# A hybrid encoder block on one core: edges that fix the written order of three engines, and tiles at multiples of 64 bytes

## The chip, the cores and the metric

The kernel runs on one core of one Trainium2 chip. The core has TensorE (PE in the profile, with its weight loads as PEld), VectorE (DVE), ScalarE (ACT), GpSimd (POOL) and SyncE (SP); each works through a queue of its own, in the order in which the compiled program lists its instructions, and they wait for each other by semaphores. The metric is the time of one execution on the device in microseconds; lower is better.

## The reference

One encoder layer over 256 positions of width 2048: four mixers side by side (a gated linear attention, a Fourier mixer, a Hyena long convolution and a short convolution), cross-attention to 256 memory rows, a SwiGLU of width 5632, with a norm before each and at the end. Nearly all the work is in the products with the weight matrices.

```python
mem_n = rms_norm(mem, mem_norm_g)
h = rms_norm(x, norm_g[l, 0])
q, k, v, g, lr, u_f, u_h, u_s = jnp.split(h @ w_in[l], split_at, axis=-1)
y_a = gla_mixer(q, k, v, g, lr, ...)
y_b = rms_norm(fnet_mixer(u_f), grp_norm_g[l, 0])
y_c = rms_norm(hyena_mixer(u_h, hy_conv_w[l], filt, hy_skip[l]), grp_norm_g[l, 1])
y_d = rms_norm(shortconv_mixer(u_s, sc_conv_w[l]), grp_norm_g[l, 2])
x = x + jnp.concatenate([y_a, y_b, y_c, y_d], axis=-1) @ w_out[l]
x = x + cross_attention(rms_norm(x, norm_g[l, 1]), mem_n, w_xq[l], w_xkv[l], w_xo[l])
x = x + swiglu(rms_norm(x, norm_g[l, 2]), w_gate_up[l], w_down[l])
return rms_norm(x, final_norm_g)

def cross_attention(h, mem_n, w_q, w_kv, w_o):
    ...
    s = jnp.einsum('bshd,bmhd->bhsm', q, k).astype(jnp.float32) * XA_HD ** -0.5
    p = jax.nn.softmax(s, axis=-1).astype(v.dtype)
    o = jnp.einsum('bhsm,bmhd->bshd', p, v).reshape(bsz, seq, D_MODEL)
    return o @ w_o

def swiglu(h, w_gate_up, w_down):
    gate, up = jnp.split(h @ w_gate_up, 2, axis=-1)
    return (jax.nn.silu(gate) * up) @ w_down
```

## The kernel before

**Numbers in two parts.** Every matrix operand is kept as a high part, rounded to a shorter format (fp32r), and a low part, the remainder. An activation slot (act0 to act23, f0 to f35, oex0 to oex3) is a tile of 128x512: the high part of 256 positions and then the low part. A product of one block of 128x128 weights is two matmuls (mm): the high weights wh with all 512 columns of the slot (L269), then the low weights wl with the 256 high ones (L270). With narrow=True the first is split in two of 256 columns (L266, L267). gemm_rows turns the roles round: the slot is the stationary operand and four blocks of wh or wl, 512 columns, stream (L321 to L323).

**The weight stream.** The blocks lie in DRAM in the order in which they are used. Stream._half takes half a slab, eight blocks: SyncE loads a slab into raw (three buffers), ScalarE casts it to wh (L89), VectorE subtracts to get wl (L90). take() calls _half at the start of every eight blocks, so that two halves more than the one in use are written ahead, or three while the pool wx is open (mixers and attention). With three buffers of wh and wl, or four, the half written then needs the buffers that TensorE has just left.

**The gemms and their order.** w_xkv for the memory's keys and values, w_in for the four mixers, w_out, then in attention() w_xq (one head of 64 blocks after the other) and w_xo, then in mlp() w_gate_up and w_down. A gemm runs over columns of 128; for each, all blocks of the inner dimension, accumulated in a bank of PSUM (psG, four banks; psM has four more for small products), and then evac(): merge() copies one half of the bank on ScalarE (L276) and adds the other on VectorE (L178), and what follows depends on the gemm. The groups that begin a gemm (first) run four or eight columns together.

**The background.** The small work between the gemms (the norms, Hyena's filters and convolutions, the gated attention, the attention heads, the loading of keys and values) is written as Python generators. Background holds them with a clock of its own: pe() adds the time of each block, dve() adds what a step gives VectorE to an account, owed, which TensorE's time pays off. After every block mm() calls poll(), and a generator whose due time has come, while owed is below 0.9, runs to its next yield; there it is due again after what is owed plus 1.3 (LAG) or a time that it names. drain() runs a generator to its end at once. So the text of the program has a definite order: the blocks, and steps of the background between them.

**Who decides the order of the queues.** The tile framework records the instructions in that order, and a scheduler then lists them for each engine. It goes by a model of times: where the next instruction of an engine isn't ready in that model, a later one that is ready may go first. Nothing in the kernel before restrains it.

**Places that the prediction speaks of.** rstd_begin multiplies squares with ones (L215), rstd_cols makes a reciprocal root in small operations on VectorE, rstd_bank scales the identity by it (dg, two operations, L244) and multiplies with ones (L246), rstd_end copies the result (rs or krs, L251). Gla.mix does this for four heads, two heads to a step: rstd_end, then a product into go, for each. head() is one attention head: scores (L637, L638), a softmax for each half of the rows, a yield, transposes (L656), a yield, the products with the values (L664, L665). load_kv fetches keys and values (mr) on GpSimd's queue and casts them (L186, L194); it is written in attention(), and so behind the w_out gemm. start_x scales x for one slot, splits it, and after every fourth multiplies the last four with a narrow matrix (L388).

Of the kernel before, what the change touches and what calls it, by code (L numbers as in the profile page):

```python
# [13 lines left out]
F32 = mybir.dt.float32  # L14
# [8 lines left out]
P = 128  # L23
# [24 lines left out]
V_SCW = 133  # L48
V_B1, V_B2, V_FR = 145, 146, 147
V_NT = 148  # L50
NV = 150

TWO_PI_1 = 6.28125
TWO_PI_2 = float(np.float32(2 * math.pi - 6.28125))
# [92 lines left out]
                self.step(e)  # L147


class Block:  # L150
    def __init__(self, ctx, tc, t):
        self.ctx, self.tc, self.nc, self.t = ctx, tc, tc.nc, t
# [66 lines left out]
    def rstd_cols(self, p, n, keep=None):  # L219

        nc = self.nc
        m = p.shape[1]
        self.bg.dve(0, 8)
        c = keep.tile([P, 24], F32, name=f"krc{next(self.kept)}") if keep else self.rp.tile([P, 24], F32, name="rc", tag="rc")
        y, v, a = (c[:, 8 * i:8 * i + m] for i in range(3))
        nc.vector.tensor_scalar(out=v, in0=p, scalar1=1.0 / n, scalar2=EPS, op0=ALU.mult, op1=ALU.add)

        nc.vector.tensor_scalar(out=a.bitcast(U32), in0=v.bitcast(U32), scalar1=1, scalar2=None, op0=ALU.logical_shift_right)
        nc.vector.tensor_scalar(out=y.bitcast(I32), in0=a.bitcast(I32), scalar1=-1.0, scalar2=float(0x5f3759df),
                                op0=ALU.mult, op1=ALU.add)  # L230
        for _ in range(3):
            self.stt(a, y, -0.5, y, ALU.mult, ALU.mult)
            self.tt(a, a, v, ALU.mult)
            self.stt(y, a, 1.5, y, ALU.add, ALU.mult)
        return y
# [95 lines left out]
    def run(self):  # L331
        nc, cp = self.nc, self.cp
        st = self.st
        self.act = [cp.tile([P, 512], F32R, name=f"act{i}") for i in range(24)]
        self.res = [cp.tile([P, 4, R], F32, name=f"res{i}") for i in range(4)]
        self.resk = lambda i: self.res[i // 4][:, i % 4, :]
        self.vec = cp.tile([P, NV], F32, name="vec")
        self.ones = cp.tile([P, P], F32, name="ones")
        self.ident = cp.tile([P, P], F32, name="ident")
        self.acc = cp.tile([P, R], F32, name="acc")  # L340

        self.kd = nc.dram_tensor("keys", (P, 16 * R), F32, kind="Internal").ap()
        self.vd = nc.dram_tensor("values", (P, 8 * 512), F32, kind="Internal").ap()
        nc.scalar.dma_start(self.vec, self.t["vecs"])
        def load(src, k, n):
            nc.sync.dma_start(self.res[k // 4][:, k % 4:k % 4 + n, :].rearrange("p k r -> p (k r)"),
                              self.t[src][:, k * R:(k + n) * R])

        self.load_x = lambda k, n: load("xT", k, n)

        warm = cp.tile([P, 1], F32, name="warm")
        nc.vector.memset(warm, 1.0)
        nc.scalar.copy(warm, warm)
        load("memT", 0, 1)
        st.after = [lambda: None, lambda: None]
        st.after += [lambda a=a: load("memT", *a) for a in ((1, 1), (2, 1), (3, 1), (4, 1), (5, 1), (6, 2), (8, 2), (10, 2), (12, 2), (14, 2))]
        nc.vector.memset(self.ones, 1.0)
        make_identity(nc, self.ident)
        with self.tc.tile_pool(name="wx", bufs=1) as st.extra:
            self.mixers()  # L360
            self.attention()
        self.mlp()
# [5 lines left out]
    def mixers(self):  # L368
        tc, nc, act = self.tc, self.nc, self.act
# [36 lines left out]
            nc.vector.tensor_reduce(out=c[:, 0:2], in_=c[:, 2:10].rearrange("p (r k) -> p r k", k=4), axis=AX.X, op=ALU.add)  # L406

        def prepare(mid):
            c = [mid.tile([P, 10], F32, name=f"sums{i}") for i in range(2)]
            yield 20  # L410
            yield from squares("mem", c[0])
            self.rcm = self.rstd_cols(c[0][:, 0:2], D, self.cp)
            yield
            self.rsm = self.rstd_end(self.rcm, 0, self.cp)
            self.bg.add(hy.filters())
            nc.sync.dma_start(gl.lrw, self.t["lrw"])
            yield from squares("x", c[1])
            col = self.rstd_cols(c[1][:, 0:2], D)
            yield
            self.rsx = self.rstd_end(col, 0, mid)  # L420
# [126 lines left out]
    def attention(self):  # L547
        tc, nc, act, st = self.tc, self.nc, self.act, self.st
        with tc.tile_pool(name="atp", bufs=1) as atp, tc.tile_pool(name="kp", bufs=1) as kp, \
                tc.tile_pool(name="mp", bufs=5) as mp:  # L550
            oex = [atp.tile([P, 512], F32R, name=f"oex{i}") for i in range(4)]
            pt = [atp.tile([P, 512], F32R, name=f"pt{i}") for i in range(2)]
            qs = atp.tile([P, 2], F32, name="qs")
            o = act[0:8] + oex + act[8:12]
            slot = lambda name, n: kp.tile([P, 512], F32R, name=name, tag=name, bufs=n)
            kv = [([], [], []) for _ in range(4)]

            def ev_q(q, p):
                q.append(slot("q", 8))
                self.split(q[-1], self.merge(p))  # L560

            def scales():

                col = self.rstd_begin([[self.acc]], D)
                nc.vector.tensor_scalar(out=qs, in0=col, scalar1=512 ** -0.5, scalar2=None, op0=ALU.mult)
                yield

            heads = []

            def load_kv():  # L570

                todo = [(hd, what, i) for hd in range(4) for what in range(2) for i in range(4)]
                parts = []

                def fetch():
                    if len(parts) < len(todo):
                        hd, what, i = todo[len(parts)]
                        m = mp.tile([P, R], F32, name="mr", tag="mr")
                        o = (4 * hd + i) * R
                        nc.gpsimd.dma_start(m, (self.vd if what else self.kd)[:, o:o + R])  # L580
                        parts.append(m)

                for _ in range(5):
                    fetch()
                yield 4
                for n, (hd, what, i) in enumerate(todo):
                    while hd > len(heads) + 1:
                        yield
                    if what == 0:
                        kv[hd][0].append(slot("kt", 8))  # L590
                        self.split(kv[hd][0][-1], parts[n])
                    else:
                        if i % 2 == 0:
                            kv[hd][1].append(slot("vh", 4))
                            kv[hd][2].append(slot("vl", 4))
                        c = slice(i % 2 * R, i % 2 * R + R)
                        self.split2(kv[hd][1][-1][:, c], kv[hd][2][-1][:, c], parts[n])
                    fetch()
                    yield 1.0

            def scores(hd, q):
                while len(kv[hd][2]) < 2:
                    yield
                yield
                yield from self.head(q, *kv[hd], pt, o[4 * hd:4 * hd + 4], qs)
                heads.append(hd)

            lp = [list(range(8)), list(range(8, 16))]
            self.bg.add(scales())
            self.bg.add(load_kv())  # L610
            gens = []
            for hd in range(4):
                q = []
                if hd > 1:
                    self.bg.drain(gens[hd - 2], True)
                self.gemm("w_xq", [(4 * hd + i) * P for i in range(4)], self.h2, lambda i, p: ev_q(q, p), first=(4, lp),
                          before=lambda n: n and hd == 0 and self.bg.drain(self.late))
                gens.append(self.bg.add(scores(hd, q)))
            h3 = self.h3 = act[12:24] + act[0:4]

            def ev_o(i, p):
                self.residual(i, p, V_NG + 32 + i, h3[i] if i < 12 else None)
                if i == 12:
                    st.extra = None

            self.gemm("w_xo", [i * P for i in range(16)], o,
                      ev_o,
                      first=(4, [list(range(12)), list(range(12, 16))]), before=lambda n: n == 1 and self.bg.drain())
            self.bg.add(self.rest(h3, 12, V_NG + 32))

    def head(self, q, kt, vh, vl, pt, o, qs):
# [10 lines left out]
        for r in range(2):  # L642
            s = self.merge(ps[r])
            self.tt(s, s, self.rsm, ALU.mult)
            c = self.rp.tile([P, 4], F32, name="rc", tag="sm")
            nc.vector.tensor_reduce(out=c[:, 0:1], in_=s, axis=AX.X, op=ALU.max)
            self.stt(c[:, 1:2], c[:, 0:1], -1.0, qs[:, r:r + 1], ALU.mult, ALU.mult)
            nc.scalar.activation(s, s, AF.Exp, scale=qs[:, r:r + 1], bias=c[:, 1:2], accum_out=c[:, 2:3])
# [591 lines left out]
```

## Time and profile before

| | us |
|---|---|
| median of 3 runs | 1525.95 |
| range of the runs | 1525.63 to 1526.79 |
| profiled execution, its own time | 1526.68 |
| span of the profiled execution, first to last instruction | 1524.6 |
| TensorE without work: to the first matmul | 4.55 |
| TensorE without work: 400 to 800 | 3.75 |
| last matmul begins | 1510.76 |

The differences between the profiled execution and its span are launch and end. In the rows in order of time the columns are start and length in us, engine, line, operation, output and inputs, shape, count, and in brackets the idle time before with what ended it. In the groups by line they are engine, operation, count, busy time, mean length in ns, and idle time before. In the list of waits they are who waited for whom, the total, how often, and the longest. A matmul's length in a row contains what overlaps with its neighbours; the pace is read from start to start.

### The profile page before, as it was taken

How to read it: one execution, taken by the hardware profiler on the slowest of the kernel's cores; microseconds unless marked ns; L12 is line 12 of the kernel's file. 1: busy time of each engine (PE TensorE's matmuls, PEld its weight loads, DVE VectorE, ACT ScalarE, POOL GpSimd, SP SyncE). 2: the span in 40 equal slices, each digit the busy share in tenths (PEclk: the TensorE clock that was granted, in tenths of full speed). 3: DMA queues.
4: the chain of work that ended last, by engine and by line, in shares of the span. 5: the costliest groups of instructions: out<-in, count | busy, mean ns of one | idle time of the engine just before them, and what ended most of it. 6: DMA issues, size and time to landing. Idle time of an engine off the chain costs nothing.

```text
span 1524.6 us, 22257 instructions
## 1 busy us (share of the span) xinstructions
PE 1502.2 (99%) x8788; PEld 1311.2 (86%) x8788; DVE 995.5 (65%) x1532; ACT 787.3 (52%) x1238; POOL 40.0 (3%) x76
## 2 busy tenths in 40 slices
PE   8999999999999999999999999999999999999996
PEld 7887788889999788888888888888888888888885
DVE  6676668678667766867766666666666664555454
ACT  6664555557445655656554444444444444444442
POOL 0100100000002000100000000000000000000000
PEclk9999999999999999999999999999999999999998
DMA  9965554354346555544545555555555555555552
GB/s 353 343 239 190 198 193 166 139 195 159 139 167 241 195 190 182 177 149 166 194 166 193 189 185 185 189 192 194 193 193 186 186 186 190 192 192 180 183 191 83
DMA packets 48808, 290.53 MB, mean 191 GB/s; under 512 B 6173, under 2 KB 7486, under 8 KB 17088
## 3 DMA queue, kind: packets, MB, share of 16 engines
q1 hardware_dynamic: 44912, 279.59, 51.5%
q0 software_dynamic: 3072, 8.39, 1.6%
q8 instruction: 69, 1.13, 0.3%
q10 hardware_dynamic: 720, 1.13, 0.2%
q14 instruction: 35, 0.29, 0.0%
HBM read 282.80 MB, written 6.29 MB: 190 GB/s over the span
## 4 chain that ended last, share of the span: by engine, by line
PE 96%; DVE 1%; DMA 1%; issue 1%; ACT 0%; SPq 0%; POOL 0%; DVEq 0%; POOLq 0%; ACTq 0%
PE pg L269 49%; PE pg L270 28%; PE pg L266 3%; PE pg L267 3%; PE pg L321 3%; PE pg L323 2%; PE pg L322 2%; PE pm L269 1%; PE pm L796 1%; DMA mr<-values 1%; PE pm L664 1%; PE pm L270 0%; PE pm L637 0%; DMA raw<-in_W 0%; DVE wl L90 0%
## 5 line engine op out<-in xcount | busy, mean ns | idle before, releaser
L269 PE MATMUL pg<-act,wh 128*128 128x512 f32 x2680 | 939.7, 394 | 8.3 <-DVE act L182 4.5
L90 DVE TENSOR_TENSOR wl<-raw,wh 128x1024 fp32r<-128x1024 f32 (+1 forms) x507 | 617.0, 1218 | 425.9 <-ACT wh L89 423.6
L270 PE MATMUL pg<-act,wl 128*128 128x256 f32 x3008 | 842.5, 281 | 0.0
L89 ACT CAST wh<-raw 128x1024 fp32r<-128x1024 f32 (+1 forms) x507 | 529.5, 1046 | 589.5 <-PE pg L269 333.4
L269 PEld LDWEIGHTS pg<-act,wh 128*128 128x128 f32 x2680 | 504.7, 188 | 120.7 <-ACT wh L89 4.5
L270 PEld LDWEIGHTS pg<-act,wl 128*128 128x128 f32 x3008 | 566.9, 189 | 2.6 <-issue 2.0
L269 PE MATMUL pg<-f,wh 128*128 128x512 f32 x540 | 191.3, 398 | 0.0
L270 PE MATMUL pg<-f,wl 128*128 128x256 f32 x576 | 161.8, 281 | 0.0
L269 PEld LDWEIGHTS pg<-f,wh 128*128 128x128 f32 x540 | 101.5, 188 | 25.2
L270 PEld LDWEIGHTS pg<-f,wl 128*128 128x128 f32 x576 | 108.8, 189 | 0.0
L266 PE MATMUL pg<-act,wh 128*128 128x256 f32 x328 | 94.8, 289 | 0.0
L267 PE MATMUL pg<-act,wh 128*128 128x256 f32 x328 | 92.1, 281 | 0.0
L178 DVE TENSOR_TENSOR tmp<-pg,tmp 128x256 f32<-128x256 f32 x183 | 76.2, 417 | 5.7 <-ACT tmp L276 5.0
L276 ACT COPY tmp<-pg 128x256 f32<-128x256 f32 x179 | 65.0, 364 | 14.6 <-PE pg L270 14.5
L321 PE MATMUL pg<-wh,act 128*128 128x512 f32 x160 | 66.4, 415 | 0.0
L323 PE MATMUL pg<-wh,act 128*128 128x512 f32 x160 | 63.3, 395 | 0.0
L322 PE MATMUL pg<-wl,act 128*128 128x512 f32 x160 | 62.9, 393 | 0.0
L266 PEld LDWEIGHTS pg<-act,wh 128*128 128x128 f32 x328 | 61.9, 189 | 0.7
L267 PEld LDWEIGHTS pg<-act,wh 128*128 128x128 f32 x328 | 61.9, 189 | 0.3
L178 DVE TENSOR_TENSOR tmp<-tmp,rs 128x256 f32<-128x256 f32 x88 | 37.3, 425 | 2.9
L321 PEld LDWEIGHTS pg<-wh,act 128*128 128x128 f32 x160 | 30.0, 188 | 10.4 <-issue 2.9
L322 PEld LDWEIGHTS pg<-wl,act 128*128 128x128 f32 x160 | 30.1, 188 | 7.5 <-issue 1.0
(233 smaller groups left out, 985.1 us busy)
## 6 DMA issues: line engine op xcount, KB each, us to landing
raw<-in_W SPq DMA_DIRECT2D x247, 1024.0 KB, 4.8
raw<-in_W SPq DMA_DIRECT2D x9, 512.0 KB, 7.3
res<-in_xT SPq DMA_DIRECT2D x8, 512.0 KB, 5.6
k<-in_mem SPq DMA_DIRECT2D x8, 256.0 KB, 9.0
k<-in_x SPq DMA_DIRECT2D x8, 256.0 KB, 8.2
keys<-tmp POOLq DMA_DIRECT2D x16, 128.0 KB, 5.7
values<-tmp POOLq DMA_DIRECT2D x16, 128.0 KB, 2.4
mr<-keys POOLq DMA_DIRECT2D x16, 128.0 KB, 3.5
```

The costliest lines, as they stand in the source:

```text
L89: nc.scalar.copy(wh[:, a:b], r[:, a:b])
L90: nc.vector.tensor_tensor(out=wl[:, a:b], in0=r[:, a:b], in1=wh[:, a:b].bitcast(F32), op=ALU.subtract)
L178: self.nc.vector.tensor_tensor(out=out, in0=a, in1=b, op=op)
L266: self.nc.tensor.matmul(p[:, 0:R], wh, slot[:, 0:R], start=start, stop=False)
L267: self.nc.tensor.matmul(p[:, 0:R], wh, slot[:, R:512], start=False, stop=False)
L269: self.nc.tensor.matmul(p[:, :], wh, slot[:, :], start=start, stop=False)
L270: self.nc.tensor.matmul(p[:, 0:R], wl, slot[:, 0:R], start=False, stop=stop)
L276: self.nc.scalar.copy(t, p[:, R:512])
L321: nc.tensor.matmul(ps[r][:, :], hi, wh, start=k == 0, stop=False)
L322: nc.tensor.matmul(ps[r][:, :], hi, wl, start=False, stop=False)
L323: nc.tensor.matmul(ps[r][:, :], lo, wh, start=False, stop=k == nk - 1)
L664: nc.tensor.matmul(p[:, :], vh[m][:, s], pt[m][:, :], start=m == 0, stop=False)
```

## The change

in_order() walks over the recorded instructions once, after the whole program has been written and before the scheduler runs. For TensorE, VectorE and ScalarE it adds an edge from each instruction to the one before it on the same engine, of a class that orders the list at compile time and makes no semaphore. The queues of GpSimd and SyncE get no such edges. DMAs that ScalarE issues count as its instructions.

The sizes of the tiles that were no multiples of 64 bytes for each partition are rounded up: vec from 600 to 640 bytes, the tiles of the reciprocal roots from 96 to 128, warm from 4 to 64, sums from 40 to 64, qs from 8 to 64, the softmax's small tile from 16 to 64. What is computed and the code around are the same.

```diff
-NV = 150
+NV = 160
...
+def in_order(tc):
+
+    last = {}
+    for i in tc.nc.cur_bb.bb.instructions:
+        e = str(i.engine)
+        if any(n in e for n in ("PE", "DVE", "Activation")):
+            if e in last:
+                tc.add_manual_dep(i, last[e].name, mybir.DependencyInfo(mybir.DependencyClass.NoSync, mybir.DependencyReason.DATA),
+                                  reason="order")
+            last[e] = i
...
-        c = keep.tile([P, 24], F32, name=f"krc{next(self.kept)}") if keep else self.rp.tile([P, 24], F32, name="rc", tag="rc")
+        c = keep.tile([P, 32], F32, name=f"krc{next(self.kept)}") if keep else self.rp.tile([P, 32], F32, name="rc", tag="rc")
...
-        warm = cp.tile([P, 1], F32, name="warm")
+        warm = cp.tile([P, 16], F32, name="warm")[:, 0:1]
...
-            c = [mid.tile([P, 10], F32, name=f"sums{i}") for i in range(2)]
+            c = [mid.tile([P, 16], F32, name=f"sums{i}") for i in range(2)]
...
-            qs = atp.tile([P, 2], F32, name="qs")
+            qs = atp.tile([P, 16], F32, name="qs")[:, 0:2]
...
-            c = self.rp.tile([P, 4], F32, name="rc", tag="sm")
+            c = self.rp.tile([P, 16], F32, name="rc", tag="sm")
...
         blk = Block(ctx, tc, t)
+        in_order(tc)
```

## The prediction

> **What bounds the kernel now.** I read the page's busy times first, then TensorE's list of waits, then the rows in order of time around each wait and around each matmul that does not belong to the weight stream.
>
> ```profile
> PE 1502.2 (99%) x8788; PEld 1311.2 (86%) x8788; DVE 995.5 (65%) x1532; ACT 787.3 (52%) x1238; POOL 40.0 (3%) x76
> ```
>
> ```profile
> PE pg L269 <- DVE act L182: 4.5, 1, 4.5
> PE pg L269 <- DVE tmp L178: 3.7, 1, 3.7
> PE pm L711 <- ACT tmp L701: 0.5, 1, 0.5
> PE pm L269 <- ACT wh L89: 0.5, 1, 0.5
> ```
>
> TensorE works for 1502.2 of 1524.6 us. It waits 4.5 us for its first operand, once 3.7 us in the middle, and hardly elsewhere; the other idle time is the tail, from the last matmul (1510.76) to 1524.6. So nothing that makes VectorE or ScalarE faster helps, and every new wait of TensorE lengthens the run by its whole length.
>
> The 3.7 us wait lies in the gemm over w_out. Its rows on ScalarE, then TensorE's:
>
> ```profile
> 495.94 0.40 ACT L194 CAST vh<-mr 128x256 fp32r<-128x256 f32 x1 [3.02 <-DMA mr<-values]
> ...
> 497.81 0.36 ACT L276 COPY tmp<-pg 128x256 f32<-128x256 f32 x1
> ```
>
> ```profile
> 494.69 0.39 PE L269 MATMUL pg<-act,wh 128*128 128x512 f32 x1
> 494.92 0.28 PE L270 MATMUL pg<-act,wl 128*128 128x256 f32 x1
> 498.94 0.79 PE L269 MATMUL pg<-act,wh 128*128 128x512 f32 x1 [3.73 <-DVE tmp L178]
> ...
> 504.67 0.40 PE L269 MATMUL pg<-act,wh 128*128 128x512 f32 x1
> ```
>
> All four banks of psG were full. The copy that begins to empty one (L276) stood in ScalarE's queue behind casts of keys and values (L186, L194), which waited for their DMA. Those casts are written in attention(), after the whole w_out gemm: the scheduler had moved them forward. After the wait TensorE ran at half its pace, a block each 0.64 us instead of 0.347, until 504.22.
>
> The second thing to see is how far VectorE departs from the written order:
>
> ```profile
> 439.07 1.27 DVE L244 TENSOR_SCALAR dg<-ident,rc 128x128 f32<-128x128 f32 x6
> ...
> 445.17 0.88 DVE L182 SCALAR_TENSOR_TENSOR go<-go,vec,rs 128x256 f32<-128x256 f32 x2
> ```
>
> Gla.mix writes, head by head, two dg, the matmul of rstd_bank (L246), the copy to rs, and the product into go. Six dg (three heads) ran 6 us before the first product, so their matmuls found everything ready. The same in Hyena's norm:
>
> ```profile
> 341.18 1.05 ACT L89 CAST wh<-raw 128x1024 fp32r<-128x1024 f32 x1 [1.48 <-PE pg L267]
> 342.16 0.59 PE L246 MATMUL pm<-dg,ones 128*128 128x256 f32 x2
> 342.26 1.22 DVE L90 TENSOR_TENSOR wl<-raw,wh 128x1024 fp32r<-128x1024 f32 x1 [1.57 <-ACT wh L89]
> ```
>
> The dg of this matmul ran at 338.87. By the program's text it comes after the subtraction L90 of 342.26.
>
> **The change, part by part.** The sum is made against the profiled execution, 1526.68 us, of which 1524.6 are the span; the median shown is 1525.95, so differences are added to that.
>
> *The w_out wait goes: -6.5.* In written order the casts for attention come after w_out. From 495.04, where the next block was due, nine blocks at 0.347 would end at 498.17; the trace has 504.67. The 16 casts and subtractions moved into the w_xq gemm (0.33 apart, some 5.3 us of either engine over two heads) are covered there: VectorE is busy 34.28 of 50 us from 550 to 600. Without that cover they would cost those 5.3.
>
> *The starts of tiles: -5.2.* The slots act are the first of their pool and whole multiples of 2048 bytes; f, wh and wl lie behind vec (600 bytes), warm (4) and the tiles of 96 bytes. Matmuls that stream f are slower than those that stream act in the same gemm:
>
> ```profile
> L269 PE MATMUL pg<-f,wh 128*128 128x512 f32 x530 | 187.8, 398 | 0.0
> ...
> L269 PE MATMUL pg<-act,wh 128*128 128x512 f32 x119 | 42.0, 392 | 0.0
> ```
>
> Start to start, a block on f takes 0.3531 us (1292.51 to 1301.69, 26 blocks) and one on act 0.3467 (899.67 to 902.79, nine). If the start is the reason, 576 blocks on f give 576 x 0.0064 = 3.7; the 64 on oex in w_xo 0.4; and the 480 matmuls of gemm_rows, which stream wh and wl at 0.70/3 = 0.2333 against two thirds of 0.3467 = 0.2311, 1.1. Its other bound is 0. I take 5.2, since the tiles that stream slowly are those that lie behind the odd sizes. The Trainium skill (SBUF — State Buffer, Specifications) gives lines of 16 bytes and names no boundary of 64; by it tiles at multiples of 16 would gain nothing and the time be 5.2 later; the rows show a difference of 6 ns, whose reason they do not show.
>
> *L246 waits for its dg: +13.8.* Background takes a step after a block; rstd_bank writes dg and the matmul in the same step. The cast of the next half (L89) and its subtraction (L90) are written at the border of eight blocks, before the step, and the cast waits until TensorE has left the last eight. From the start of that cast it is 1.08 to L90 (341.18 to 342.26), 1.14 to the next operation of VectorE, 0.48 for two dg and 0.37 from VectorE to TensorE (a scaling ended at 606.73, its transposes began at 607.10): 3.1 us. Each matmul now waits 3.1 less its distance from that cast, by the places where TensorE ran it: 63.92 (cast 63.35) 2.5; 97.48 (95.97) 1.6; 342.16 2.1; 443.64 (441.96) 1.4; 449.54 (448.60) 2.2; 464.58 (463.96) 2.5; 783.10 (781.50) 1.5; at 429.31 VectorE is free and nothing is waited for. Behind the waiting matmul stands the whole stream. Bounds: 0, if VectorE comes to dg first as at 429.31, and 9 x 3.1 = 28.
>
> *The second head of a pair: +3.6.* In written order its dg follow the product of the first head, which waits for the copy. From the first matmul 0.63 to its copy (443.64 to 444.27), 0.38, 0.48, 0.48 and 0.37 are 2.3; the first pair of matmuls itself takes 0.5. Two pairs at 1.8.
>
> *Transposes in head(): +7.2.* After its score matmuls the step charges VectorE 2 x (0.42 + 0.42 + 0.16) = 2.0 and is due again 2.0 + 1.3 later, so the transposes are written some 3.4 after the scores' end. Rows 128 to 255 now follow all of rows 0 to 127 on VectorE: twice 0.42 + 0.42 + 0.41 + 0.16 + 0.79 (the exponential on ScalarE with its read) + 0.17 + 0.35 = 2.7 from 601.69, with 0.4 of handovers and the 0.37, is 607.9 against 602.63 + 3.4 = 606.0.
>
> ```profile
> 602.35 0.28 PE L638 MATMUL pm<-kt,q 128*128 128x256 f32 x1
> ...
> 606.52 0.38 PE L656 MATMUL pm<-ident,tmp 128*128 128x128 f32 x2
> 607.10 0.38 PE L656 MATMUL pm<-ident,tmp 128*128 128x128 f32 x2
> ```
>
> Four heads at 1.8; bounds 0 and 4 x 3.
>
> *start_x: +4.4.* The matmuls L388 need the x scaled just before them. VectorE did this early (183.31); as written it follows L90 (183.70, then 1.14), a scaling, cast and subtraction of the slot before: 0.40 + 0.41 + 0.40 more, then 0.48 and 0.37, so 186.9 against 185.63 for the last of them. Four at 1.1; bounds 0 and 8.
>
> *Start and rest: +2.4.* At 7.91 four L269 ran ahead of their L270; now each L270 waits for its wl, 0.4 (0 to 0.7). The other 25 or so places where a background matmul follows VectorE or ScalarE have one or two due times between; I take 2 (0 to 8). The tail has one chain in either order: 0. The edges bring no semaphore: 0.
>
> Sum: -6.5 - 5.2 + 13.8 + 3.6 + 7.2 + 4.4 + 2.4 = +19.7; 1526.68 + 19.7 = 1546.4, or by the median **1546**.
>
> **The rivals.** *VectorE is early enough (faster).* The background's own clock (LAG 1.3, owed below 0.9) spaces dependent steps, and VectorE is idle for 35% of the span. If each first L246 falls late in its eight blocks, at 2.5 of 2.77 us, it waits 0.6: 7 x 0.6 with 3.6 for the pairs is 7.8, against 11.7 gained: 1522; with half of the pairs' wait, 1520. It decides as soon as all waits together stay below 11.7. For it: no bound excludes small waits. Against: of the seven places six lie within 1.7 us of the cast.
>
> *Nothing is reordered.* If the edges do not bind the queues, only the tiles' starts are left: 1521 with their gain, 1526 without. Against it: the six dg above could be nothing but reordered.
>
> *Weights come late (slower still).* In gate_up the evacuation of an odd group now stands before the cast: copy 0.42 after the group's end, three operations of VectorE 0.46 apart to 1.79, a cast, L89 to 3.18, L90 to 4.44; the half is needed 16 x 0.347 = 5.55 after. A chain over 5.55 would cost its excess 44 times; 0.5 of it gives 22 more, 1568. Against: 1.1 us in hand.
>
> *The clock falls at the pairs.* Waits of 1.4 to 2.2 and 1.8 with 0.5 of work between could bring back the half pace, whose eight blocks cost 8 x 0.293 = 2.3 at 499 to 504: 1551 for two. No row has such a pattern, so it stays in the range. The Trainium skill (TensorE: Matmul & The Clock Gate, Why this matters for your kernels) puts the danger at gaps above some 3 us; the row of 3.73 agrees, and by it no single wait here would do it.
>
> **How the numbers follow.** Forecast 0.57, faster rival 0.25, nothing reordered 0.08, late weights 0.10 (the clock within the first). The forecast's own range is 1533 to 1559. For 8 in 10 the whole range goes from 1516, which takes in most of the faster rival, to 1560, leaving late weights and a twentieth at either end out. A measurement tells 0.2%, 3.05 us, from no change: below 1522.9 lie the faster rival and part of the unreordered case, 0.28; within 0.2% 0.07; above 1529.0 0.65.
>
> **What would show it.** Right: TensorE waits at L246 for dg, seven times or more, and at L656 and L388; no wait at w_out's fifth column, and the casts of mr after 573; f and act at the same pace. Wrong: TensorE's waits sum to under 12 us, or its new wait is for wl (L90), or blocks on f still take 0.353.

## The result and the profile after

The changed kernel takes 1595.25 us (median of five runs, 1590.74 to 1598.41) beside 1525.95 us for the kernel before, a ratio of 1.0452 with an interval of 1.0433 to 1.0471. It is 69.3 us slower. The forecast was slower, but 1546 us, and its range ended at 1560.

The profiled execution took 1593.36 us, 1591.5 of them the span. All lines of the changed file behind in_order() are 12 higher than before: L246 is now L258, L244 is L256, L656 is L668, L388 is L400, L269 and L270 are L281 and L282. The busy times of the engines in the kernel after:

```profile
PE 1533.4 (96%) x8788; PEld 1325.8 (83%) x8788; DVE 1012.0 (64%) x1532; ACT 787.8 (49%) x1236; POOL 40.1 (3%) x76
```

TensorE has the same 8788 matmuls, and yet it is busy 31.2 us longer and idle 35.7 us longer (58.1 against 22.4). So there are two losses, not one: it waits more, and it works more slowly while it works. TensorE's list of waits in the kernel after gives the first; its largest lines:

```profile
PE pm L258 <- DVE dg L256: 15.7, 9, 2.1
PE pm L668 <- DVE tmp L662: 9.9, 6, 2.3
PE pm L400 <- DVE tmp L194: 5.9, 7, 1.9
PE pg L281 <- DVE act L194: 5.0, 2, 4.7
PE pg L281 <- ACT wh L89: 3.0, 2, 2.1
PE pg L282 <- DVE wl L90: 1.7, 3, 0.8
...
```

The list has three new lines at the top (dg, transposes, start_x), then the first operand's wait, which was there before, and two lines for weights that come late. What is missing is the wait of 3.7 us for tmp in the w_out gemm. The work of load_kv now stands where it is written. The casts of its tile mr, with shortest, median and longest length in ns and the start of the first and the last, in the kernel before and then in the kernel after:

```profile
L186 ACT CAST kt<-mr x16: 396/407/410, 481.9 to 627.2; 128x256 fp32r<-128x256 f32 x16
L194 ACT CAST vh<-mr x16: 397/405/415, 484.3 to 641.8; 128x256 fp32r<-128x256 f32 x16
```

```profile
L198 ACT CAST kt<-mr x16: 387/400/408, 616.3 to 704.4; 128x256 fp32r<-128x256 f32 x16
L206 ACT CAST vh<-mr x16: 397/401/408, 629.7 to 714.3; 128x256 fp32r<-128x256 f32 x16
```

The second loss has several parts; one of them shows where TensorE waits for nothing. Between 900 and 1000 us both kernels run w_gate_up, only L269 and L270 on act. The windows' rows (length, TensorE's busy time and number of matmuls, granted clock, DMA share, GB/s) are, for the kernel before and then for the kernel after:

```profile
900.00:1000.00 100.00, 100.00 (x579) 1.00 0.53 190
```

```profile
900.00:1000.00 100.00, 100.00 (x572) 1.00 0.53 187
```

At full clock and without a gap, seven matmuls fewer fit into 100 us. Start to start a block (two matmuls) on act takes 0.351 us on the mean where it took 0.347.

### The profile page after: what moved, and what is told of

The parts are those of the page before. It is cut to its first block, busy times and chain, and to the rows that moved or that the text cites. A ratio compares the mean times of both kernels' runs of the same rounds, so it can differ in the third digit from the quotient of the medians.

```text
span 1591.5 us, 22237 instructions
## 1 busy us (share of the span) xinstructions
PE 1533.4 (96%) x8788; PEld 1325.8 (83%) x8788; DVE 1012.0 (64%) x1532; ACT 787.8 (49%) x1236; POOL 40.1 (3%) x76
## 4 chain that ended last, share of the span: by engine, by line
PE 87%; DVE 6%; ACT 4%; issue 2%; DMA 0%; SPq 0%; DVEq 0%; ACTq 0%
PE pg L281 45%; PE pg L282 25%; PE pg L278 3%; PE pg L279 2%; PE pg L333 2%; ACT wh L89 2%; DVE wl L90 2%; PE pg L334 2%; PE pg L335 2%; DVE tmp L190 1%; PE pm L808 1%; PE pm L281 1%; PE pm L258 0%; DMA raw<-in_W 0%; DVE tmp L194 0%
## 5 line engine op out<-in xcount | busy, mean ns | idle before, releaser
L281 PE MATMUL pg<-act,wh 128*128 128x512 f32 x2680 | 953.4, 397 | 5.9 <-DVE act L194 5.0
L282 PE MATMUL pg<-act,wl 128*128 128x256 f32 x3008 | 853.4, 284 | 0.9 <-DVE wl L90 0.9
L90 DVE TENSOR_TENSOR wl<-raw,wh 128x1024 fp32r<-128x1024 f32 (+1 forms) x507 | 606.2, 1217 | 327.4 <-ACT wh L89 326.1
L89 ACT CAST wh<-raw 128x1024 fp32r<-128x1024 f32 (+1 forms) x507 | 519.8, 1040 | 213.8 <-PE pg L281 118.7
L281 PEld LDWEIGHTS pg<-act,wh 128*128 128x128 f32 x2680 | 505.6, 189 | 125.2 <-ACT wh L89 5.9
L282 PEld LDWEIGHTS pg<-act,wl 128*128 128x128 f32 x3008 | 569.2, 189 | 3.4 <-DVE wl L90 2.0
L281 PE MATMUL pg<-f,wh 128*128 128x512 f32 x540 | 193.0, 401 | 2.1 <-ACT wh L89 2.1
L282 PE MATMUL pg<-f,wl 128*128 128x256 f32 x576 | 162.8, 283 | 0.9 <-DVE wl L90 0.8
L281 PEld LDWEIGHTS pg<-f,wh 128*128 128x128 f32 x540 | 102.2, 189 | 27.4 <-ACT wh L89 2.4
L282 PEld LDWEIGHTS pg<-f,wl 128*128 128x128 f32 x576 | 109.7, 190 | 1.6 <-DVE wl L90 1.5
L278 PE MATMUL pg<-act,wh 128*128 128x256 f32 x328 | 96.8, 295 | 0.0
L279 PE MATMUL pg<-act,wh 128*128 128x256 f32 x328 | 93.6, 285 | 0.0
L198 ACT CAST f<-tmp 128x256 fp32r<-128x256 f32 x36 | 14.6, 407 | 50.8 <-DVE tmp L190 50.8
L202 ACT ACTIVATE act<-res,vec 128x256 fp32r<-128x256 f32 x48 | 23.8, 506 | 31.9 <-DVE res L190 31.1
```

The lines of the kernel that those rows point to most:

```text
L89: nc.scalar.copy(wh[:, a:b], r[:, a:b])
L90: nc.vector.tensor_tensor(out=wl[:, a:b], in0=r[:, a:b], in1=wh[:, a:b].bitcast(F32), op=ALU.subtract)
L202: self.nc.scalar.activation(slot[:, 0:R], src, AF.Copy, scale=g)
L278: self.nc.tensor.matmul(p[:, 0:R], wh, slot[:, 0:R], start=start, stop=False)
L279: self.nc.tensor.matmul(p[:, 0:R], wh, slot[:, R:512], start=False, stop=False)
L281: self.nc.tensor.matmul(p[:, :], wh, slot[:, :], start=start, stop=False)
```

## The experiments

Each experiment was timed against runs of the kernel before on the same chip, whose median was between 1526.9 and 1528.0 us.

**The two halves of the change.** edges_only has in_order() and the old sizes; sizes_only has the sizes and not in_order().

```diff
# edges_only
+        in_order(tc)
# sizes_only
-NV = 150
+NV = 160
...
-            qs = atp.tile([P, 2], F32, name="qs")
+            qs = atp.tile([P, 16], F32, name="qs")[:, 0:2]
```

> The edges alone, tiles where they were. Theory A (the edges make TensorE wait, the equal starts of tiles slow its pace): waits at L246, L656 and L388 as after the whole change, some 32 us, and about 10 us of lost clock, less 6.5 for w_out, so 1570 to 1580, with blocks on act still 0.347 apart. Rival B (the starts are a gain, as predicted, and the pace is slow because of the edges): 1597 to 1602, blocks on act at 0.351.

> The tile sizes alone, no edges. Theory A: the weights and the slots now begin at the same place modulo 64 bytes and every block takes 0.351 to 0.353 instead of 0.347: some 3000 blocks x 0.0045 = 13.5 us, 1538 to 1544, the wait in w_out still there. Rival B (the starts as predicted): 1519 to 1523, blocks on f at 0.347. Rival C (no effect): 1526.

Measured: edges_only 1586.96 us (ratio 1.0393, 1.0379 to 1.0407), sizes_only 1536.97 (1.0067, 1.0054 to 1.0079), before 1526.96. The edges cost 60.0 and the sizes 10.0, and their sum of 70.0 is, within the spread of the runs, the whole of the 69.3. Both are losses. The sizes, forecast as a gain, slow the blocks on act from 0.347 to 0.351 us and leave those on f at 0.353.

**The edges engine by engine.** edges_pe orders TensorE alone, edges_dveact VectorE and ScalarE alone.

```diff
# edges_pe
-        if any(n in e for n in ("PE", "DVE", "Activation")):
+        if any(n in e for n in ("PE",)):
# edges_dveact
-        if any(n in e for n in ("PE", "DVE", "Activation")):
+        if any(n in e for n in ("DVE", "Activation")):
```

> Edges on TensorE alone, tiles where they were. If the waits come from VectorE's and ScalarE's order, dg and the like are early again and TensorE waits little at L246 and L656: 1524 to 1534, the wait in w_out still there. If TensorE's own order makes them, about as much as with all edges, 1565 to 1580.

> Edges on VectorE and ScalarE alone, TensorE free to take later blocks first. The casts for attention stay behind w_out, so its wait goes (-6.5). If TensorE's going round is all that keeps it from waiting: 1517 to 1528. If the late dg holds it up in either order: 1535 to 1580.

Measured: edges_pe 1540.18 us (1.0087, 1.0067 to 1.0107), edges_dveact 1562.34 (1.0231, 1.0217 to 1.0245). The largest waits of edges_dveact, and that for dg:

```profile
PE pg L281 <- ACT wh L89: 6.9, 7, 2.1
PE pg L281 <- DVE act L194: 6.0, 3, 4.6
PE pg L282 <- DVE wl L90: 5.1, 8, 0.8
...
PE pm L258 <- DVE dg L256: 0.3, 1, 0.3
```

The wait for dg, 15.8 us with all edges, is 0.3 here and absent in edges_pe: it needs both orders at once. With only VectorE and ScalarE bound, the scheduler let TensorE run weight blocks past the matmul that waits (the second dg of the first pair starts at 68.1, and TensorE runs blocks until its matmul at 68.54). With only TensorE bound, VectorE made dg early, six of them in a row from 439.28 as in the kernel before. The largest waits left with VectorE and ScalarE bound are for weights that come late, 12 us of them. They are not the whole of the 35.4 us: TensorE is idle 15.8 us longer than before and busy 19.8 us longer, and most of the latter isn't traced. In edges_pe two waits have come, 4.7 us for acc and 3.8 for the transposes. The wait in w_out is still there in edges_pe (4.3) and down to 1.4 in edges_dveact.

**Where weights and slots begin.** The starts of the tiles, from the compiled programs: before, act begins at 0 modulo 64, the weights wh and wl at 32, f and oex at 32. After, all of them begin at 0. w_shift32 makes the weights begin at 0 too, by one unused tile of 32 bytes, which GpSimd fills once; slots_shift32 leaves the weights and moves f, oex and pt in the same way.

```diff
# w_shift32
+        self.gap = pool("gap", 1).tile([P, 8], F32, name="gap")
+        tc.nc.gpsimd.memset(self.gap, 0.0)
         rawp = pool("rawp", 3)
# slots_shift32
+            gap = atp.tile([P, 8], F32, name="gap")
+            nc.gpsimd.memset(gap, 0.0)
             oex = [atp.tile([P, 512], F32R, name=f"oex{i}") for i in range(4)]
...
+            gap2 = fp.tile([P, 8], F32, name="gap2")
+            nc.gpsimd.memset(gap2, 0.0)
             f = act[4:12] + [fp.tile([P, 512], F32R, name=f"f{i}") for i in range(36)]
```

> The kernel before with one unused tile of 32 bytes ahead of the weight buffers: raw, wh, wl and what lies behind them move by 32 bytes, so that weights and slots now all begin at multiples of 64; no size is changed and no order. Theory A (a block is slow where its weights and its slot begin at the same place modulo 64): act blocks go from 0.3467 to about 0.351 us each, f blocks stay at 0.353, and the time is that of the sizes alone, 1534 to 1539 us, ratio 1.005 to 1.008. Rival B (the sizes themselves, or small tiles on shared lines, made the 10 us): act blocks stay at 0.3467 and the time is within 2 us of before.

> The kernel before with 32 unused bytes ahead of f and ahead of oex and pt: weights stay at 32 modulo 64, and all slots begin at 0. Theory A: the f blocks of w_down go from 0.353 to 0.3467 us, 576 of them by 0.0063 = -3.6, and the oex blocks of w_xo by another -0.4: 1522 to 1524 us beside 1526 to 1527, ratio 0.9970 to 0.9980. Rival B (the f blocks are slow for another reason, such as their distance from the weights or the load on VectorE and ScalarE there): f blocks stay at 0.353, no change.

Measured: w_shift32 1538.66 us (1.0081, 1.0067 to 1.0094), slots_shift32 1522.73 (0.9974, 0.9966 to 0.9983), before 1526.89. The same windows, 900 to 1000 in w_gate_up and 1360 to 1460 in w_down (blocks on act and, mostly, f), for before, w_shift32 and slots_shift32:

```profile
900.00:1000.00 100.00, 100.00 (x579) 1.00 0.53 190
1360.00:1460.00 100.00, 100.00 (x570) 1.00 0.52 185
```

```profile
900.00:1000.00 100.00, 100.00 (x572) 1.00 0.54 190
1360.00:1460.00 100.00, 100.00 (x568) 1.00 0.52 184
```

```profile
900.00:1000.00 100.00, 100.00 (x578) 1.00 0.53 190
1360.00:1460.00 100.00, 100.00 (x579) 1.00 0.52 189
```

An unused tile of 32 bytes costs 11.8 us when it brings the weights to the place of act modulo 128, and two of them gain 4.2 us when they take f and oex away from the place of the weights. w_shift32 changes no size, so the 10.0 us of sizes_only need no other cause than the starts. By the pace, 2680 blocks on act at 4.0 ns more (346.8 to 350.8, the table below) are 10.7 us, an estimate from the traces.

**How fine the rule is.** f_three_shifts and f_nine_steps put 32 bytes more ahead of every twelfth or fourth f, so that one column of w_down streams slots at several places.

```diff
# f_three_shifts; f_nine_steps has "if i and i % 4 == 0"
-            f = act[4:12] + [fp.tile([P, 512], F32R, name=f"f{i}") for i in range(36)]
+            f = act[4:12]
+            for i in range(36):
+                if i % 12 == 0:
+                    gap = fp.tile([P, 8], F32, name=f"gap{i}")
+                    nc.gpsimd.memset(gap, 0.0)
+                f.append(fp.tile([P, 512], F32R, name=f"f{i}"))
```

> The kernel before with 32 unused bytes ahead of f0, of f12 and of f24: f0 to f11 begin 32 bytes off the weights modulo 64, f12 to f23 64 bytes off (the same place modulo 64, another modulo 128), f24 to f35 96 bytes off. Theory A, with 64 as the step: blocks on f0 to f11 and on f24 to f35 take 0.3467 us, those on f12 to f23 0.351 to 0.353. Rival B (the step is 128 or more): only an offset of 0 is slow, and all three thirds take 0.3467. One look, for the pace of the blocks by slot; the time should come out some 2.4 us below before under A and 3.6 under B.

> The kernel before with 32 unused bytes ahead of f4, f8, f12 and so on: f0 to f3 begin at the place of the weights modulo 256, each next four 32 bytes further, f32 to f35 again at an offset of 0. So far offsets of 32 and 160 gave 0.3467 us a block, 0 gave 0.353, and 64, 96 and 128 gave 0.351. Theory A' (the step is 128 and only 32 past the weights is fast): 32 and 160 fast, all others slow. Rival B' (what counts is the slot's own place: fast where the slot is at a multiple of 128 and the weights are not): here the slots at multiples of 128 are those at offsets 32 and 160, so the same; a second kernel with the weights moved would tell these apart. Rival C (64 and 96 were slow in f_three_shifts for their place late in the loop over k and not for their offset): then 64 and 96, at positions 16 to 23 here, are fast.

Measured, as mean of start to start over the groups of four f in a column: f_three_shifts has 347.0, 346.7 and 346.5 ns at 32 bytes off the weights; 347.3, 353.8 and 352.2 at 64; 352.5, 350.0 and 349.7 at 96. f_nine_steps, from 0 on in steps of 32, has 351.7, 348.8, 347.3, 350.0, 349.6, 347.7, 347.9, 350.0, 352.5. Single runs took 1525.74 and 1525.78 us. The slow blocks at 96 in f_three_shifts speak against a step of 64. f_nine_steps bears out neither Theory A' (64 and 192 are as fast as 32 and 160) nor Rival C (64 is fast, but 96 is not). Groups of one place differ among themselves (at 64 from 347.3 to 353.8). A part of that is the grouping: in the kernel before, blocks on f repeat 349, 350 and 361 ns, so that means of four spread from 351.7 to 355.3 at one place. Whether what went before in the column plays a part too was not told apart. Three kernels with one place each for all f settle it better.

```diff
# f_shift64; f_shift96 and f_shift128 have 24 and 32 in place of 16
+            gap2 = fp.tile([P, 16], F32, name="gap2")
+            nc.gpsimd.memset(gap2, 0.0)
             f = act[4:12] + [fp.tile([P, 512], F32R, name=f"f{i}") for i in range(36)]
```

> The kernel before with 64 unused bytes ahead of f: all f slots begin 64 bytes off the weights. One look, for the pace of the f blocks within a column of w_down. Theory A (64 is the step: the same place modulo 64 is slow): 0.351 to 0.353 us a block. Rival (only 0 and 128 modulo 256 are slow; the slow blocks at 64 in f_three_shifts were carried over from a change of place within the column): 0.3467.

> The same with 96 bytes: all f slots begin 96 off the weights. Theory A (the place modulo 64 decides, 96 is as good as 32): 0.3467 us a block. Rival (the step is 128 and only 32 past the weights is at full pace): 0.350.

> The same with 128 bytes, the place that act has in the changed kernel (0.351 us there). Theory A: 0.351 to 0.353. Rival (f is slow only where it begins at the same place modulo 256, act in the changed kernel for another reason): 0.3467.

Single runs took 1525.72, 1525.72 and 1525.01 us.

| start of the slot behind that of the weights, modulo 256 | kernel | ns a block |
|---|---|---|
| 0 | before, f | 353.0 |
| 32 | slots_shift32, f | 346.7 |
| 64 | f_shift64, f | 349.1 |
| 96 | f_shift96, f | 350.1 |
| 128 | f_shift128, f | 351.2 |
| 128 | after, act | 350.8 |
| 160 | before, act | 346.8 |

Theory A with a step of 64 falls: 64 lies between what it and its rival said, and 96 is slow. Slots that begin 32 bytes past the weights modulo 128 are the fastest; all other places tried as a whole are slower, 0 the most. 192 and 224 were seen only in the mixed column.

Rival B' of f_nine_steps stays open: that a block is fast where its slot begins at a multiple of 128 and its weights do not. The weights stood at two places only, at 224 modulo 256 before and at 0 after and in w_shift32, while act stood at 128. With the weights at 224, the slots 32 and 160 behind them are just those at 0 and 128. For the distance speaks that both places of the weights give nearly the same pace at 0 (353.0, and 353.3 for f in sizes_only) and at 128 (351.2 and 350.8). No kernel had the weights at 0 and the slots 32 behind them, which would decide it.

**The wait in w_out by itself.** kv_hold has one part of the edges: the ScalarE casts of load_kv may not go ahead of the last ScalarE instruction written before attention().

```diff
+            self.held = []
+            mark = [i for i in self.seen() if "Activation" in str(i.engine)][-1]
             self.attention()
+            for i in self.held:
+                self.tc.add_manual_dep(i, mark.name, mybir.DependencyInfo(mybir.DependencyClass.NoSync, mybir.DependencyReason.DATA),
+                                       reason="hold")
...
+                    n0 = len(self.seen())
...
+                    self.held += [j for j in self.seen()[n0:] if "Activation" in str(j.engine)]
```

> The kernel before with a part of the edges alone: the ScalarE casts of load_kv (kt and vh) may not be ahead of the last ScalarE instruction written before attention(); nothing else is ordered. Theory A (the wait of TensorE in w_out is ScalarE standing at a cast of mr that the planner put ahead of the residual of w_out, as the prediction has it): the wait of 3.7 us and the half pace behind it go, -5 to -6.5 us: 1520 to 1522 beside 1526 to 1527, ratio 0.9957 to 0.9967. Rival B (what stands in ScalarE is something else, or the casts are missed at the start of attention): the wait stays, or a new one for kt comes in its place, and the time is within 1 us of before or above it.

Measured: 1520.23 us (0.9961, 0.9949 to 0.9974) beside 1526.89. TensorE's whole list of waits in kv_hold:

```profile
PE pg L269 <- DVE act L182: 4.6, 1, 4.6
PE pm L721 <- ACT tmp L711: 0.5, 1, 0.5
```

Only the wait at the start and the one at the end are left; the half pace at 499 to 504 is gone with its wait, and no wait for keys comes in its place. The 6.7 us are the forecast's 6.5.

**The waits for dg, and the casts.** edges_dg_ahead is edges_only with dg written behind the chain that makes y, ahead of the yields, so that only the matmul stands behind them. edges_free_casts is edges_only without edges for the casts to wh and wl. edges_both has both.

```diff
# edges_dg_ahead, one of the places
...
         box["col"] = self.rstd_begin([[acc]], n, keep)
+        dg = self.rstd_dg(box["col"])
         for _ in range(wait):
             yield
-        box["rs"] = self.rstd_end(box["col"], 0, keep)
+        box["rs"] = self.rstd_end(dg, keep)
# edges_free_casts; free holds the names of the casts
...
-        if any(n in e for n in ("PE", "DVE", "Activation")):
+        if i.name not in free and any(n in e for n in ("PE", "DVE", "Activation")):
```

> All edges, sizes as before, and dg's two VectorE instructions are written directly behind the chain that makes y, a yield or two ahead of the matmul of rstd_bank that needs them. Theory A (L246 waits for dg because the edges put that matmul directly behind VectorE instructions that still stand behind other work): of edges_only's 1587 go the nine waits (15.8), the matmul that no longer overlaps at each (about 0.45 x 9 = 4) and the half pace behind those at 69 and 470 to 490 (3 to 7): 1560 to 1567. Rival B (VectorE is late as a whole; dg written earlier only stands in its order ahead of other work): the waits turn up at the next operation, for act, tmp or wl, and the time stays above 1575.

> All edges but those of the weight stream's casts (wh on ScalarE, wl on VectorE), which the planner places as before. Theory A (the waits for wh and wl at the first groups of w_gate_up and w_down are casts that the edges hold behind the evacuations of a whole group): 1.8 us at 856 and 2.8 at 1388 go, with 0.8 at 339, about 1 at the start, and the half pace behind 1388 (2 to 4): 1577 to 1581 beside edges_only's 1587. Rival B (casts let free are put ahead of the evacuations and make these late): the waits for wh and wl go and waits for the evacuations take their place, 1585 or more.

> All edges, with dg written ahead of its matmul and the weight stream's casts left free, together. Alone they took 19.1 and 21.5 us off edges_only's 1587. edges_free_casts still had 8.9 us of waits for dg, 2.2 of lost overlap and 3.4 of half pace behind them. Theory A (mostly different waits): 1565.4 - 8.9 - 2.2 - 3.4 = 1551, in 1547 to 1555; what is then left over before is the waits in head(), in start_x and for acc. Rival B (the same waits twice): 1560 to 1565.

Measured: edges_dg_ahead 1567.84 us (1.0259, 1.0243 to 1.0275) and edges_free_casts 1565.44 (1.0254, 1.0240 to 1.0268) beside 1527.32; edges_both 1557.08 (1.0185, 1.0162 to 1.0208) beside 1527.96. The first waits of edges_dg_ahead, where the line for dg is gone and the others stand nearly as in edges_only:

```profile
PE pm L672 <- DVE tmp L666: 10.1, 6, 2.3
PE pm L401 <- DVE tmp L194: 5.9, 7, 1.8
PE pg L282 <- DVE act L194: 5.0, 2, 4.6
PE pg L282 <- ACT wh L89: 3.5, 3, 2.1
```

That is the mechanism of Theory A; the 19.1 us gained are just short of its range, which began at 20 (1567). edges_free_casts gained 21.5 where 6 to 10 were expected; its first waits:

```profile
PE pm L261 <- DVE dg L259: 8.9, 5, 2.1
PE pm L671 <- DVE tmp L665: 8.4, 4, 2.9
PE pg L284 <- DVE act L197: 4.6, 1, 4.6
PE pm L403 <- DVE tmp L197: 4.4, 2, 2.2
PE pm L230 <- DVE acc L193: 3.9, 2, 2.0
```

The lines for wh and wl have shrunk as expected, but so has that for dg, from nine waits to five. A subtraction of the weight stream is what dg stood behind on VectorE at 67.00 to 68.14 in edges_only (rows below), so letting casts and subtractions go can shorten both. The wait for acc has grown from 0.4 us to 3.9. The two remedies overlap in part: edges_both took 29.9 off, not 36 (Theory A) nor 22 to 27 (Rival B). The 29 us by which it stays behind the kernel before were not taken apart further.

**What beats both.** hold_and_shift has kv_hold and slots_shift32 together.

> kv_hold and slots_shift32 together: load_kv's ScalarE casts stay behind the mixers, and f, oex and pt begin 32 bytes off the weights. The two act in different stages, so the gains should add: 6.7 and 4.2 measured alone, 1526.9 - 10.9 = 1516, in 1514 to 1518, ratio 0.992 to 0.994. If they overlapped (a block that runs at the faster pace asks for weights that are not there), 1518 to 1521 with new waits for wh or wl in w_down.

Measured: 1516.25 us (1515.94 to 1516.87), a ratio to before of 0.993 (0.9918 to 0.9943). The two add: 11.1 us, where they gained 6.7 and 4.2 alone. The busy times of hold_and_shift:

```profile
PE 1495.9 (99%) x8788; PEld 1310.3 (87%) x8788; DVE 994.5 (66%) x1532; ACT 786.9 (52%) x1238; POOL 40.1 (3%) x78
```

TensorE is busy 6.3 us less than before (1502.2) with the same matmuls, and idle 18.6 us of the span where it was 22.4.

## Why the prediction was right and wrong

**The w_out wait: right.** Forecast -6.5, measured by itself -6.7, by the mechanism that was named: casts of keys and values in ScalarE's queue ahead of the residual.

**The starts of tiles: the step that failed by its sign.** The prediction put -5.2; the sizes cost 10.0. It had seen rightly that f streams more slowly than act (0.3531 against 0.3467), and took the tiles that begin at an odd place for the cause: "the tiles that stream slowly are those that lie behind the odd sizes". The weights lie behind them too. What the runs showed instead is that both starts count, the slot's and the weights': before, act was the fast one because it began elsewhere than the weights, and f the slow one because it began where they do. Rounding every tile to 64 bytes did not bring f to the pace of act, but act to the pace of f. The rows of before could not tell an odd start from an equal one; with both bounds at 0 or a gain, the range had no room for a loss. The part of 1.1 for gemm_rows came to almost nothing: three of its matmuls take 0.704 us before and 0.702 in sizes_only. The sentence about the Trainium skill's page SBUF — State Buffer, section Specifications (lines of 16 bytes, no boundary of 64), spoke against the gain; by it a shift of 32 bytes would change nothing, and w_shift32's 11.8 us and slots_shift32's -4.2 show that it changes the time.

**The waits: right in place, the sum too small.** The list of waits of edges_only beside the terms:

| term of the prediction | forecast | edges_only |
|---|---|---|
| L246 for dg, with the second head of a pair | 13.8 + 3.6 | 15.8 |
| transposes in head() | 7.2 | 10.1 |
| start_x | 4.4 | 5.9 |
| start and rest | 2.4 | 10.0 |

Nine waits for dg came, at the places named, of 1.3 to 2.1 us. The first of them in edges_only, in rows of ScalarE, VectorE and TensorE:

```profile
65.92 1.05 ACT L89 CAST wh<-raw 128x1024 fp32r<-128x1024 f32 x1
...
67.00 1.22 DVE L90 TENSOR_TENSOR wl<-raw,wh 128x1024 fp32r<-128x1024 f32 x1 [0.37 <-ACT wh L89]
68.14 0.47 DVE L256 TENSOR_SCALAR dg<-ident,krc 128x128 f32<-128x128 f32 x2
68.76 1.03 PE L258 MATMUL pm<-dg,ones 128*128 128x256 f32 x2 [2.11 <-DVE dg L256]
...
74.13 0.63 PE L281 MATMUL pg<-act,wh 128*128 128x512 f32 x1
```

Cast, subtraction, dg, matmul: 2.84 us from the cast, where the prediction counted 3.1. In head() the second and the third head wait twice in a row (1.2 and 2.3, 1.0 and 2.3), not once; start_x waits at each group of four, and in three of the four twice. Its term was also summed low: the prediction's own 186.9 against 185.63 gives 1.3 for a group and 5.1 in all. The last term was mis-sized: it allowed 2 us for some 25 small places, and there are 7.1 us of waits for wh and wl alone. The rival with late weights had looked at w_gate_up's pairs, where in fact nothing is late; 4.6 of the 7.1 us come where the group of columns that begins w_gate_up or w_down ends (at 856 and 1388) and its evacuations, written together, stand ahead of the casts. In edges_only, at the first four columns of w_down:

```profile
1386.14 0.42 ACT L713 ACTIVATE tmp<-res 128x256 f32<-128x256 f32 x1 [0.95 <-DVE res L190]
...
1387.01 2.93 ACT L89 CAST wh<-raw 128x1024 fp32r<-128x1024 f32 x3
...
1388.09 0.49 PE L281 MATMUL pg<-f,wh 128*128 128x512 f32 x1 [2.07 <-ACT wh L89]
1389.35 0.38 PE L282 MATMUL pg<-f,wl 128*128 128x256 f32 x1 [0.77 <-DVE wl L90]
```

Three casts queue up behind the evacuations (L713) and run back to back, and TensorE has run out of weights before the first is done.

**The clock: seen, and priced at next to nothing.** The prediction kept it out of the sum and in the range, at 2.3 us for each of two pairs. Summing (1 - granted clock) over windows of 10 us, the kernel before loses 8.3 us and edges_only 23.1. Of these 4.9 and 6.0 lie behind the last matmul, where no work waits for the clock, and the other 3.4 of before go with the w_out wait. So the edges lose up to 17.1 us that way. Two windows of edges_only, behind the wait of 2.11 us at 68.76 and around one of 2.14 at 107.79:

```profile
70.00:80.00 10.00, 10.00 (x42) 0.71 0.69 270
100.00:110.00 10.00, 7.86 (x42) 1.00 0.51 190
```

The one is followed by blocks 0.64 us apart until 75.41 (the row of 74.13 above is one of them), the other by none. The clock also fell behind waits of 1.8 (196.19 to 198.03) and 2.0 us (472.38 to 474.37), before a second one of 0.7 or 1.5 had more than begun, and at pairs of 1.7 and 1.5, 1.2 and 2.3, 1.0 and 2.3, 2.1 and 0.8. In the kernel after it fell at 100 to 110 and not at 70. The Trainium skill (TensorE: Matmul & The Clock Gate, Why this matters for your kernels) puts the danger at gaps above some 3 us, and the prediction wrote that by it no single wait here would do it; the wait of 2.11 us did.

What tells waits of one length apart is how they lie on a grid in time. In edges_only the seven falls ahead of the tail come at 68.94, 198.64, 475.12, 488.77, 673.09, 707.23 and 1389.89, whole multiples of 3.413 us apart, and the clock stays at half for one or two such steps. The steps around the two waits, with the half clock behind the first:

```profile
65.53:68.94 3.41, 1.30 (x8) 1.00 1.04 417
68.94:75.77 6.83, 6.83 (x19) 0.50 1.01 405
```

```profile
103.07:106.49 3.42, 2.58 (x16) 1.00 0.00 1
106.49:109.90 3.41, 2.11 (x9) 1.00 0.85 280
```

The first wait lies within one step, of which TensorE is idle for 62%; the second is cut in two, 25% of one step and 38% of the next. In edges_only every fall ends a step that was idle for 54% or more, and no other step at full clock between the first 10 us and the tail is idle for more than 43%. In the other traces the border lies near a half too, with single exceptions (a fall after 39% in edges_both, none after 54% in edges_free_casts).

**The account.** -6.7 for w_out, 41.8 for the new waits, 17.1 for the clock are 52.2 of the edges' 60.0. The other 7.8 are not traced one by one; a part is overlap. In the stream the next matmul begins 0.11 to 0.12 us into one of 0.28 (66.03 and 66.14 in edges_only), so that some 0.16 of it costs nothing; ahead of a wait it does. 0.16 at each of some 38 new waits are 6 us, an estimate. With the sizes' 10.0 this is 70, against a forecast of 19.7: of the difference 15.2 are the starts of tiles, 17.1 the clock, 7.6 the waits for weights and other small ones, and the rest, some 10, transposes, start_x and overlap. Without the 15.2 the time would be 1580, without the 17.1 it would be 1578, both beyond the range's 1560: several steps failed at once, of which only the starts had the wrong sign.

**The signs to look for.** Waits at L246, L656 and L388, none in w_out, and casts of mr late: all came. f and act at one pace came as well, but at the slow one; blocks on f still take 0.353, which the prediction had named as a sign against it.

## What to carry to other kernels

A stall of the bounding engine costs more than its length: here 42 us of short waits brought up to 17 us of half clock and, by an estimate, 6 of lost overlap, so a list of waits is a lower bound. When some streams are faster than others, compare both operands' starts, not one: a few unused bytes ahead of a pool moved the pace of the blocks on its slots or weights by 1 to 2%. A written order is a good tool for the one instruction that a scheduler moves to a harmful place (-6.7 us), and a bad one for whole queues, unless the text itself writes each operand well ahead of its use; with dg written ahead and the casts free, 29 of the 60 us were still there.

## What the runs showed of the hardware that was not expected

The pace of an fp32r block depends on where the streamed slot and the stationary weights begin: 346.7 ns with the slot 32 and 346.8 with it 160 bytes behind the weights modulo 256, 349.1 at 64, 350.1 at 96, 351 at 128, 353.0 at 0. In w_gate_up of the kernel after, TensorE is busy all the time at a granted clock of 1.00, so the profile's busy share shows nothing of it; counts of matmuls in a window and start-to-start times do. Why just these places is open, as is Rival B': no run told whether it is the loading of the next weights beside the stream.

The granted clock fell to half after single waits of TensorE as short as 1.8 us (behind the one at 196.19 in edges_only, or at 100.88 in edges_free_casts), and not after some longer ones. The falls lie on a grid of 3.413 us, and in edges_only a fall follows the steps in which TensorE was idle for more than half, and no others. Each fall shows as 1.7 us lost, or twice that (70 to 80: 2.9, with 0.5 in the window before).
